# The first net's fifth chunk made by seven block products, and activations dealt without steps

## The chip, the cores and the metric

The kernel runs on one core of a Trainium2 chip. The metric is the device time of one execution in microseconds; what counts is the median over several runs. Five engines work side by side: TensorE (PE) multiplies matrices, VectorE (DVE) and ScalarE (ACT) do elementwise work, GpSimd (POOL) a little of everything, and SyncE (SP) issues nearly all loads from memory in one queue.

## The reference

Two layers of a mixed network over 256 tokens of width 1024, in float32. Each layer has two gated nets ("ffn1" and "ffn2"), a mixer and a cross attention, each with a layer norm behind it. The change is in the four gated nets.

```python
def swiglu(x, w_gate, w_up, w_down):
    return (jax.nn.silu(x @ w_gate) * (x @ w_up)) @ w_down

for l in range(DEPTH):                                       # DEPTH = 2
    h = layer_norm(ALPHA * h + 0.5 * swiglu(h, ffn1_gate[l], ffn1_up[l], ffn1_down[l]), ln_g[l, 0], ln_b[l, 0])
    ...                                                      # mixer: layer_norm(ALPHA * h + mix)
    h = layer_norm(ALPHA * h + cross_attn(h, mem, ...), ln_g[l, 2], ln_b[l, 2])
    h = layer_norm(ALPHA * h + 0.5 * swiglu(h, ffn2_gate[l], ffn2_up[l], ffn2_down[l]), ln_g[l, 3], ln_b[l, 3])
```

The gate and up weights are 1024 x 2816, the down weights 2816 x 1024.

## The kernel before

**Precision by parts.** Every float32 operand of a large product is split into a high part (rounded by a copy on ScalarE) and a low part (the difference, on VectorE): `split`, lines 60 to 62. A product is then three matrix products, high by high, high by low, low by high (`mm_rows`, line 130; each goes through `product`, line 106). A tile of 1024 weight elements per partition thus costs one copy and one subtraction (line 62) before PE can use it. There are eight buffers each for high and low weights ("whi", "wlo") and three for raw weights as loaded ("raw").

**A gated net** (`ffn`, from line 377). The 2816 hidden columns are made in six chunks, five of 512 and one of 256. For a chunk of 512, `hidden` makes all products of x with the gate weights and with the up weights: 2 tiles of 128 tokens x 8 blocks of 128 rows x 2 matrices x 3 parts = 96 products of 512 columns. `activate` (line 402) applies silu on ScalarE, `gated` (line 406) multiplies on VectorE. `turn` (line 410) brings the result, which has tokens on partitions, to hidden columns on partitions: four loads deal it from tile "sg" to tile "dealt" in groups of 32 partitions, and VectorE turns blocks of 32 x 32 (line 418), once for each tile of tokens, before they are split. The chunk's down products follow later: `both(c, u)` adds half u of chunk c, 24 products, to the sums in "dn". Behind chunk c come `both(c - 2, 1)` and `both(c - 1, 0)`; the last three halves are in `tail`, in front of the layer norm in `finish`.

**Seven products** (`by_seven`, line 515). In the second, third and fourth net, chunk 3 is made otherwise. Gate and up weights of the chunk form, with x, a product of 2 x 2 blocks, and this is made with seven block products of 12 instead of eight: 84 products of 512 columns. It needs sums of weight blocks (line 544, VectorE, in place, four sums of two pieces), each split as above, 14 splits in all; differences of the four quarters of x (`blocks_of_x`, lines 499 to 513), which are kept in the tiles of the attention's keys (kTh, kTl); and sums and differences of the results (`put`, line 566). The quarters and later block 00 of the weights lie in the tile "spare" of 2048 elements, block 01 in the tiles of the layer norm's scale and offset ("lng", "lnb"), blocks 11 and 10 in raw buffers. The quarters are made behind chunk 1, two chunks before they are used.

**The first net** has no chunk by seven (`sevens` is empty). Behind its chunk 1 it loads the small parameters and the cross attention's memory (`beginnings`, on POOL's queue), and behind its chunk 2 it turns the memory and computes with the parameters (`later`, lines 191 and 257); the tiles of the memory (tag "m") and of parameters are its own.

**Order of work.** Only a few stretches have an order written by hand: the start of the first net on PE, VectorE and ScalarE, and a part of the mixer. Elsewhere a planner goes through the instructions by the order in which the code emits them, and may take one that is ready earlier than one that is not; a tile is given to its next user when its last reader is done. `issue_after` queues a load or an instruction behind another one of its engine.

**Layouts of tokens.** `transposed` (line 173) turns h on PE with the unit matrix `idn`, or in one place `jdn`, which also reverses the tokens.

Of the kernel before, what the change touches and what calls it, by code (L numbers as in the profile page):

```python
# [46 lines left out]
def model(ctx: ExitStack, tc: tile.TileContext, t: dict, out: bass.AP):  # L47
# [16 lines left out]
    def load(src, k0, nk, c0, ncol, fine=False, strewn=False):  # L64

# [4 lines left out]
        for a in range(k0, k0 + nk, step):  # L70
# [4 lines left out]
            for b in range(0, step, part):  # L75
                loads.append(nc.sync.dma_start(
                    raw[:, b : b + part, :],
                    src[:, c0 : c0 + ncol].rearrange("(p k) c -> p k c", p=P)[:, a + b : a + b + part, :]
                    if strewn
                    else src[(a + b) * P : (a + b + part) * P, c0 : c0 + ncol].rearrange("(k p) c -> p k c", p=P),  # L80
                ))
# [71 lines left out]

    jdn = cst.tile([P, P], F32, name="jdn")
# [24 lines left out]
    def load_memory(mp, behind):  # L179
        m = [mp.tile([P, 4, 8, 32], F32, tag="m", name="m", bufs=2) for _ in range(2)]  # L180
# [23 lines left out]
    rows = cst.tile([P, P], F32, name="rows")  # L204
# [10 lines left out]
    def small_parameters(op):  # L215
        nc.gpsimd.memset(rows, 0.0)
# [13 lines left out]
        mf = op.tile([P, NT, len(narrow), 64], F32, name="mf", bufs=1)  # L230
# [61 lines left out]
    def finish(mm, y, scale, gb, last=False, flip=False):  # L292
# [6 lines left out]
        for i in range(NT):  # L299
# [8 lines left out]
            for c in pieces:  # L308
                n = c.start // 512
                v = halves(h[i][:, c])  # L310
                if len(pieces) == 3 and n:
                    o = acc((P, 256))
                    mm(i, n, slice(c.start - 512, c.stop - 512), o, None)
                    nc.vector.tensor_tensor(v, v, sums(o), op=ALU.add)  # L314
                else:
                    mm(
                        i, n, slice(0, 512), None,
                        None if last or not i or not n else lambda: transposed(h[0], 0, xTh, xTl),
                    )
                    nc.vector.scalar_tensor_tensor(v, v, ALPHA / scale, sums(y[i][n]), op0=ALU.mult, op1=ALU.add)  # L320
# [19 lines left out]
        return lambda: transposed(h[1], 1, xTh, xTl, jdn if flip else idn)  # L340

    def project_back(slabs, late, gb, scale, between=lambda: None):
# [30 lines left out]
        return finish(tail, y, scale, gb)  # L373


    def ffn(l, name, n, pend=None, last=False, early=None):
        gate, up, down = (t[f"{name}_{x}"][l] for x in ("gate", "up", "down"))
        with tc.tile_pool(name="ffn", bufs=2, reuse_waits="tile") as fp:
# [21 lines left out]

            def activate(s, i, og):
                nc.scalar.activation(halves(s[:, i, :]), sums(og), AF.Silu)

            def gated(s, i, ou):
                v = halves(s[:, i, :])
                nc.vector.tensor_tensor(v, sums(ou), v, op=ALU.mult)
# [4 lines left out]
            def turn(s):  # L411
# [4 lines left out]
                for i in range(NT):  # L416
                    d = fp.tile([P, 4, P], F32, tag="up", name="square")
                    nc.vector.transpose(  # L418
                        d.rearrange("p k (i b) -> p b k i", b=4), x[:, :, i, :].rearrange("p b (j k) -> p b k j", k=4)
# [4 lines left out]
            def first():  # L424
# [5 lines left out]
                if pend is None:  # L430
# [8 lines left out]
                    with tc.manual_schedule(engines={E.Activation, E.DVE, E.PE}):  # L439
# [8 lines left out]
                        transposed_half(h[0], 0, 0, xTh, xTl)  # L448
                        busy(1)
                        split(*wg.todo[0])  # L450
                        transposed_half(h[0], 0, 1, xTh, xTl)
# [3 lines left out]
                        transposed_half(h[1], 1, 0, xTh, xTl)  # L455
                        group(1, 0)
                        split(*wg.todo[2])
                        transposed_half(h[1], 1, 1, xTh, xTl)
# [56 lines left out]
            def by_seven(c0, bx):  # L515
                def quarter(m, j, halves_of):
                    for b, r in enumerate(halves_of):
                        n = r.shape[1]
                        k = 4 * j + b * n
                        loads.append(nc.sync.dma_start(  # L520
                            r, m[k * P : (k + n) * P, c0 : c0 + CHUNK].rearrange("(k p) c -> p k c", p=P)
                        ))
                    return [r[:, 2 * h : 2 * h + 2, :] for h in range(2) for r in halves_of[:1]] if n == 4 else halves_of

# [3 lines left out]
                def raw():  # L528
                    return rows_by_columns(wp.tile([P, 2048], F32, tag="raw", name="raw", bufs=3))

                w00 = quarter(gate, 0, [rows_by_columns(
                    fp.tile([P, 4, 4 * P], F32, tag="spare", name="sum", bufs=1).rearrange("p n c -> p (n c)")
                )])
                w01 = quarter(up, 0, [
                    rows_by_columns(wp.tile([P, DM], F32, tag=g, name="raw")) for g in ("lng", "lnb")
                ])
                w11 = quarter(up, 1, [raw()])
                w10 = quarter(gate, 1, [raw()])

                def parts_of(r, plus=None):  # L540
                    hi, lo = [], []
                    for i in range(2):
# [4 lines left out]
                        h, w = (x.rearrange("p (k c) -> p k c", c=CHUNK) for x in (h, w))  # L547
# [14 lines left out]
                def half_sum():  # L562
                    return halves(fp.tile([P, 4, P], F32, tag="up", name="half").rearrange("p k t -> p (k t)"))

                def put(o, a, op, b):
                    nc.vector.tensor_tensor(o, a, b, op=op)

                s = activations()
                g = [halves(s[:, i, :]) for i in range(NT)]
                o = [acc((P, CHUNK)) for _ in range(4)]  # L570
                run(o[0], part_of_x(0, 0), parts_of(w00))
                nc.scalar.copy(g[0], sums(o[0]))
# [3 lines left out]
                put(e, sums(o[1]), ALU.add, g[0])  # L576
                run(o[3], bx[2], parts_of(w01, w11))
                put(g[1], sums(o[3]), ALU.add, e)
                f = half_sum()
                put(f, sums(o[2]), ALU.subtract, g[1])  # L580
                put(e, sums(o[2]), ALU.subtract, e)
# [4 lines left out]
                m = acc((P, CHUNK))  # L586
                run(m, part_of_x(1, 1), parts_of(w00, w10))
                put(g[1], sums(m), ALU.add, g[1])
                nc.scalar.activation(g[1], g[1], AF.Silu)
                put(g[1], g[1], ALU.mult, f)  # L590
                m = acc((P, CHUNK))
                run(m, bx[3], parts_of(w11))
                put(e, sums(m), ALU.add, e)
                put(g[0], g[0], ALU.mult, e)
                return turn(s)

            def last_hidden(c0):
# [11 lines left out]
                split(ah[:, 0:2, :], al[:, 0:2, :], s)  # L609
                return ah, al  # L610

            def slab(c, u):
                if c < len(chunks) - 1:
                    w = load(down[c * CHUNK : (c + 1) * CHUNK], 2 * u, 2, 0, DM, strewn=True)
                else:
                    w = load(down, c * 4, 2, 0, DM)
# [4 lines left out]
            sevens = (3,) if early is None else ()  # L621
# [17 lines left out]
            for c, (c0, ncol) in enumerate(chunks):  # L639
# [33 lines left out]
            return finish(tail, ys, 0.5, gb, last=last, flip=name == "ffn1")  # L673
# [27 lines left out]
    def mixer(l, fill):  # L701
        w_in = t["w_in"][l]
        with tc.tile_pool(name="mix", bufs=1, reuse_waits="tile") as mp:
# [284 lines left out]
            return project_back([slab(a) for a in (0, 6, 2, 4)], 3, gb, 1.0)  # L988


    def attention(l, pend):
        scale = (DM // HEADS) ** -0.5
        with tc.tile_pool(name="att", bufs=1, reuse_waits="tile") as ap:
# [108 lines left out]
            return project_back([slab(a) for a in (0, 2, 4, 6)], 3, gb, 1.0, others)  # L1102
# [40 lines left out]
```

## Time and profile before

| | us |
|---|---|
| median of 3 runs | 1081.59 (1081.54 to 1081.89) |
| profiled execution | 1082.44 |
| its span | 1080.7 |
| PE busy in it | 1071.4 |
| VectorE busy | 908.4 |
| ScalarE busy | 592.8 |

The profile shows one execution. "PE" lines are matrix products; a product of 512 columns is shown with about 380 ns, but the next one starts 216 ns after it, since they are pipelined. "busy" in a window is the time in which at least one instruction of the engine ran. In a line of a group, the two figures behind the bar are the total busy time and the mean duration in ns; then come idle time in front of the group and who ended it. Line numbers are those of the kernel before.

### The profile page before, as it was taken

How to read it: one execution, taken by the hardware profiler on the slowest of the kernel's cores; microseconds unless marked ns; L12 is line 12 of the kernel's file. 1: busy time of each engine (PE TensorE's matmuls, PEld its weight loads, DVE VectorE, ACT ScalarE, POOL GpSimd, SP SyncE). 2: the span in 40 equal slices, each digit the busy share in tenths (PEclk: the TensorE clock that was granted, in tenths of full speed). 3: DMA queues.
4: the chain of work that ended last, by engine and by line, in shares of the span. 5: the costliest groups of instructions: out<-in, count | busy, mean ns of one | idle time of the engine just before them, and what ended most of it. 6: DMA issues, size and time to landing. Idle time of an engine off the chain costs nothing.

```text
span 1080.7 us, 15689 instructions
## 1 busy us (share of the span) xinstructions
PE 1071.4 (99%) x6015; PEld 947.5 (88%) x6015; DVE 908.4 (84%) x1198; ACT 592.8 (55%) x828; POOL 61.0 (6%) x113
## 2 busy tenths in 40 slices
PE   9999999999999999999999999999999999999997
PEld 7888888989899888888888888898898998888886
DVE  6678677998988898998697998798989889889885
ACT  6456553766457455556365465456764664645650
POOL 9500001000000000000000000010000000000000
PEclk9999999999999999999999999999999999999999
DMA  9986764754476387288468459656536664773761
GB/s 325 289 293 203 249 223 153 237 196 165 167 263 204 123 295 269 96 275 286 156 234 282 166 166 329 229 165 241 174 122 231 240 228 154 255 253 109 260 236 39
DMA packets 122715, 231.86 MB, mean 215 GB/s; under 512 B 6352, under 2 KB 45552, under 8 KB 117520
## 3 DMA queue, kind: packets, MB, share of 16 engines
q1 hardware_dynamic: 120848, 228.48, 63.1%
q0 software_dynamic: 1216, 1.20, 0.4%
q10 hardware_dynamic: 576, 1.18, 0.3%
q8 instruction: 47, 0.77, 0.3%
q14 instruction: 28, 0.23, 0.1%
HBM read 216.15 MB, written 1.05 MB: 201 GB/s over the span
## 4 chain that ended last, share of the span: by engine, by line
PE 99%; DMA 0%; DVE 0%; issue 0%; DVEq 0%
PE acc L106 65%; PE dn L106 30%; PE acc L170 1%; PE dn L845 1%; DMA h<-in_x_dram 0%; PE dn L904 0%; PE dn L903 0%; PE dn L893 0%; PE acc L969 0%; PE dn L810 0%; PE dn L437 0%; DVE h L334 0%; DVE h L330 0%; DVE st L322 0%; DVE h L314 0%
## 5 line engine op out<-in xcount | busy, mean ns | idle before, releaser
L62 DVE TENSOR_TENSOR wlo<-raw,whi 128x1024 fp32r<-128x1024 f32 (+1 forms) x390 | 460.8, 1207 | 91.0 <-ACT whi L61 81.1
L61 ACT CAST whi<-raw 128x1024 fp32r<-128x1024 f32 (+1 forms) x390 | 391.2, 1040 | 258.3 <-PE dn L106 128.4
L106 PE MATMUL acc<-whi,xT 128*128 128x512 f32 x1192 | 359.7, 380 | 0.0
L106 PEld LDWEIGHTS acc<-whi,xT 128*128 128x128 f32 x1192 | 225.2, 189 | 32.1
L106 PE MATMUL acc<-wlo,xT 128*128 128x512 f32 x596 | 225.9, 379 | 0.0
L106 PE MATMUL acc<-xT,whi 128*128 128x512 f32 x576 | 142.1, 382 | 0.0
L106 PE MATMUL dn<-whi,ah 128*128 128x512 f32 x346 | 131.5, 380 | 0.0
L106 PE MATMUL dn<-wlo,ah 128*128 128x512 f32 x346 | 131.2, 379 | 0.0
L106 PE MATMUL dn<-whi,al 128*128 128x512 f32 x346 | 131.1, 379 | 0.0
L106 PEld LDWEIGHTS acc<-wlo,xT 128*128 128x128 f32 x596 | 112.7, 189 | 15.7
L106 PEld LDWEIGHTS acc<-xT,whi 128*128 128x128 f32 x576 | 104.1, 190 | 11.8
L106 PE MATMUL dn<-whi,xT 128*128 128x512 f32 x288 | 88.8, 382 | 0.0
L106 PEld LDWEIGHTS acc<-xT,wlo 128*128 128x128 f32 x576 | 75.5, 191 | 3.9
L106 PE MATMUL acc<-xT,wlo 128*128 128x256 f32 x576 | 75.9, 275 | 0.0
L106 PEld LDWEIGHTS dn<-wlo,ah 128*128 128x128 f32 x346 | 65.4, 189 | 9.5 <-DVE wlo L62 0.3
L106 PEld LDWEIGHTS dn<-whi,al 128*128 128x128 f32 x346 | 65.4, 189 | 9.3
L106 PEld LDWEIGHTS dn<-whi,ah 128*128 128x128 f32 x346 | 65.4, 189 | 9.1
L418 DVE STREAM_TRANSPOSE square<-dealt 128x512 f32<-128x512 f32 x40 | 62.8, 1645 | 3.8 <-DMA dealt<-sg 3.8
L327 POOL TENSOR_TENSOR rs<-rs,nhalf 128x1 f32<-128x1 f32 x16 | 14.9, 928 | 846.3 <-DVE rs L326 846.3
L106 PEld LDWEIGHTS dn<-whi,xT 128*128 128x128 f32 x288 | 54.7, 190 | 7.8 <-DVE xT L62 0.3
L106 PE MATMUL dn<-wlo,xT 128*128 128x512 f32 x144 | 54.8, 381 | 0.0
L61 ACT CAST ah<-square 128x512 fp32r<-128x512 f32 x40 | 24.6, 619 | 39.7 <-DVE square L418 39.7
(227 smaller groups left out, 1174.0 us busy)
## 6 DMA issues: line engine op xcount, KB each, us to landing
raw<-in_ffn_down_dram SPq DMA_DIRECT2D x44, 1024.0 KB, 5.4
raw<-in_ffn_up_dram SPq DMA_DIRECT2D x41, 1024.0 KB, 6.1
raw<-in_ffn_gate_dram SPq DMA_DIRECT2D x39, 1024.0 KB, 5.1
raw<-in_w_in_dram SPq DMA_DIRECT2D x24, 1024.0 KB, 5.0
dealt<-sg SPq DMA_DIRECT2D x80, 128.0 KB, 3.8
raw<-in_ca_k_dram SPq DMA_DIRECT2D x8, 1024.0 KB, 4.9
raw<-in_w_out_dram SPq DMA_DIRECT2D x8, 1024.0 KB, 4.8
raw<-in_ca_v_dram SPq DMA_DIRECT2D x8, 1024.0 KB, 5.4
```

Of the source, the lines that this page charges most:

```text
L61: nc.scalar.copy(hi, src)
L62: lows.append(nc.vector.tensor_tensor(lo, src, hi.bitcast(F32), op=ALU.subtract))
L106: nc.tensor.matmul(o, w, x, start=start, stop=stop)
L170: nc.tensor.transpose(pt[:, k, :], src[:, (4 * j + k) * P : (4 * j + k + 1) * P], unit)
L327: nc.gpsimd.tensor_tensor(rs, rs, nhalf[:, 0:1], op=ALU.pow)
L418: nc.vector.transpose(d.rearrange("p k (i b) -> p b k i", b=4), x[:, :, i, :].rearrange("p b (j k) -> p b k j", k=4))
L845: nc.tensor.matmul(o[g, hh, :], kc[:, hh, g], x, start=True, stop=True)
```

## The change

1. Chunk 4 of the first net is made by seven products too. The quarters of x for it are made behind chunk 3. The layer norm's scale and offset are loaded behind chunk 5 there, since block 01 uses their tiles.
2. Three tiles of 1024 elements, "spare0" to "spare2", take the place of the tile "spare", the two of the memory and those of the parameters. The quarters and block 00 lie in "spare0" and "spare1"; block 10 lies in "dealt" and "spare2" and no longer in a raw buffer. Every block is loaded as two pieces of 512 KB. The products with blocks 11 and 10 change places, and the gated result of such a chunk is written to "spare2".
3. The silu and the gating write their result with groups of 32 columns in the order in which they are dealt, in two instructions for each tile of tokens where there was one; dealing and turning then read and write 32 elements in a row where they went in steps of four. The down weights are loaded in whole blocks of 128 rows, without the interleaving (`strewn`) that answered to those steps.
4. In exchange the tokens of a tile stand in another order within a net: x is turned with `pdn`, a permuted unit matrix, which POOL copies from `idn` at the start; behind a first net of a layer `jdn` and `idn` are used as before. The chunk of 256 is brought to the same order in its split, in two instructions each where there was one.

```diff
-    def load(src, k0, nk, c0, ncol, fine=False, strewn=False):
+    def load(src, k0, nk, c0, ncol, fine=False):
...
+    pdn = cst.tile([P, P], F32, name="pdn")
+    nc.gpsimd.tensor_copy(pdn.rearrange("p (r b) -> p b r", b=4), idn.rearrange("p (b r) -> p b r", b=4))
...
-        m = [mp.tile([P, 4, 8, 32], F32, tag="m", name="m", bufs=2) for _ in range(2)]
+        m = [
+            mp.tile([P, DM], F32, tag=f"spare{n}", name="m", bufs=1).rearrange("p (k b j) -> p k b j", k=4, j=32)
+            for n in range(2)
+        ]
...
+            def ordered(v):
+                return v.rearrange("p (a k j) -> p k a j", a=4, j=32)
+
+            def by_two(v, o):
+                o = o.rearrange("p (n a j m) -> p m n a j", n=2, a=4, m=2)
+                return [(ordered(v)[:, 2 * m : 2 * m + 2], o[:, m]) for m in range(2)]
+
             def activate(s, i, og):
-                nc.scalar.activation(halves(s[:, i, :]), sums(og), AF.Silu)
+                for v, o in by_two(s[:, i, :], og):
+                    nc.scalar.activation(v, o, AF.Silu)
 
             def gated(s, i, ou):
-                v = halves(s[:, i, :])
-                nc.vector.tensor_tensor(v, sums(ou), v, op=ALU.mult)
+                for v, o in by_two(s[:, i, :], ou):
+                    nc.vector.tensor_tensor(v, o, v, op=ALU.mult)
...
                     nc.vector.transpose(
-                        d.rearrange("p k (i b) -> p b k i", b=4), x[:, :, i, :].rearrange("p b (j k) -> p b k j", k=4)
+                        d.rearrange("p k (b r) -> p b k r", b=4), x[:, :, i, :].rearrange("p b (k j) -> p b k j", k=4)
                     )
...
-                d = fp.tile([P, 4, 4 * P], F32, tag="spare", name="quarters", bufs=1)
-                q = [d[:, n, :].rearrange("p (k t) -> p k t", t=P) for n in range(4)]
+                d = [fp.tile([P, DM], F32, tag=f"spare{n}", name="quarters", bufs=1) for n in range(2)]
+                q = [d[n // 2].rearrange("p (n k t) -> p n k t", n=2, t=P)[:, n % 2] for n in range(4)]
...
+                w00 = block(gate, 0, pieces("spare0", "spare1"))
+                w01 = block(up, 0, pieces("lng", "lnb"))
+                w11 = block(up, 1, whole())
+                w10 = block(gate, 1, pieces("dealt", "spare2"))
...
-                m = acc((P, CHUNK))
-                run(m, part_of_x(0, 1), parts_of(w10))
-                put(g[0], sums(m), ALU.add, g[0])
-                nc.scalar.activation(g[0], g[0], AF.Silu)
...
+                o = [acc((P, CHUNK)) for _ in range(3)]
+                run(o[0], bx[3], parts_of(w11))
+                put(e, o[0], ALU.add, e)
+                run(o[1], part_of_x(0, 1), parts_of(w10))
+                put(g[0], o[1], ALU.add, g[0])
+                run(o[2], part_of_x(1, 1), parts_of(w00, w10))
+                put(g[1], o[2], ALU.add, g[1])
+                s = fp.tile([P, NT, CHUNK], F32, tag="spare2", name="sg", bufs=1)
+                for i, u in enumerate((e, f)):
+                    v = ordered(s[:, i, :])
+                    nc.scalar.activation(v, g[i].rearrange("p (k a j) -> p k a j", a=4, j=32), AF.Silu)
+                    nc.vector.tensor_tensor(v, v, u.rearrange("p (k a j) -> p k a j", a=4, j=32), op=ALU.mult)
...
-            sevens = (3,) if early is None else ()
+            sevens = (3,) if early is None else (4,)
...
-                if c == 1 and sevens:
+                if sevens and c == (1 if early is None else min(sevens) - 1):
                     bx = blocks_of_x()
                 if c == (max(sevens) + 1 if sevens else 1):
-
-                    with tc.issue_after(loads[-1].ins) if early is not None else nullcontext():
-                        gb = ln_params(l, n)
-                        rest = early(fp) if early is not None else ()
+                    gb = ln_params(l, n)
+                if c == 1 and early is not None:
+
+                    with tc.issue_after(loads[-1].ins):
+                        rest = early(fp)
```

More of the change, by code (lines that the diff above doesn't have):

```diff
@@ L215, in small_parameters @@
     def small_parameters(op):
+        spare = op.tile([P, DM], F32, tag="spare2", name="rows", bufs=1)
+        rows = spare[:, 0:P]
         nc.gpsimd.memset(rows, 0.0)
@@ L290, in ln_params, with finish @@
         return g, b
-    def finish(mm, y, scale, gb, last=False, flip=False):
+    def finish(mm, y, scale, gb, units, last=False):
         g, b = gb
@@ L317, in finish @@
                         i, n, slice(0, 512), None,
-                        None if last or not i or not n else lambda: transposed(h[0], 0, xTh, xTl),
+                        None if last or not i or not n else lambda: transposed(h[0], 0, xTh, xTl, units[0]),
                     )
@@ L339, in finish, with project_back @@
                     e.dma_start(out[0, tok(i), c], h[i][:, c])
-        return lambda: transposed(h[1], 1, xTh, xTl, jdn if flip else idn)
-    def project_back(slabs, late, gb, scale, between=lambda: None):
+        return lambda: transposed(h[1], 1, xTh, xTl, units[1])
+    def project_back(slabs, late, gb, scale, unit, between=lambda: None):
         y = [[acc((P, 512), "dn") for _ in range(2)] for _ in range(NT)]
```

94 lines of the change are left out of this document (40 added, 54 removed).

## The prediction

> **What bounds the kernel now.** I read the engine totals first, then the chain that ended last, then the chain in order of time.
>
> ```profile
> span 1080.7 us, 15689 instructions
> PE 1071.4 (99%) x6015; PEld 947.5 (88%) x6015; DVE 908.4 (84%) x1198; ACT 592.8 (55%) x828; POOL 61.0 (6%) x113
> ```
> ```profile
> 107.95 10.36 PE dn L106 x48
> 118.31 20.72 PE acc L106 x96
> 139.03 10.36 PE dn L106 x48
> ...
> 450.92 18.13 PE acc L106 x84
> ...
> 639.45 10.56 PE dn L106 x48
> ```
>
> TensorE (PE) is the whole chain. In 118.31 to 139.03, the first net's chunk 4, 96 products take 20.72 us, 0.216 us each; the chunk by seven products in the second net, at 450.92, has 84 and takes 18.13 us, the same 0.216 us. So nothing is gained unless PE gets fewer products, and everything else costs only where it makes PE wait. The one wait behind a chunk by seven is in the third net: its 48 products at 639.45 take 10.56 us where 10.36 is usual.
>
> Who could make PE wait is seen in the windows of the same stages (each engine: busy us, and count):
>
> ```profile
> 86.20:107.95 21.75, 21.75 (x102) 19.06 (x101) 21.04 (x37) 15.88 (x20) 0.00 (x0) 1.00 0.53 185
> 107.95:118.31 10.36, 10.36 (x50) 9.07 (x49) 7.51 (x7) 4.36 (x5) 0.00 (x0) 1.00 0.97 319
> 118.31:139.03 20.72, 20.72 (x98) 18.14 (x97) 12.47 (x13) 10.27 (x12) 0.00 (x0) 1.00 0.60 200
> 433.95:450.92 16.97, 16.97 (x80) 14.88 (x79) 16.87 (x16) 6.31 (x6) 0.00 (x0) 1.00 0.30 93
> 450.92:469.05 18.13, 18.13 (x85) 15.88 (x85) 18.13 (x20) 11.44 (x14) 0.00 (x0) 1.00 0.48 160
> ```
>
> The third pair of figures is VectorE (DVE). During a chunk by seven it works 18.13 of 18.13 us, and before it 16.87 of 16.97 us: it starts on the chunk's weights 17 us ahead of PE and only just arrives. In the first net it is free for 0.71 us in 86.20 to 107.95, for 2.85 in 107.95 to 118.31, and for 8.25 in 118.31 to 139.03. So the question is whether the first net's DVE can get its work done before PE asks for it.
>
> **The products.** 96 products become 84: -2.59 us on the chain, sure as far as PE is fed.
>
> **DVE per operation.** The rows by shape (busy us, mean ns):
>
> ```profile
> L418 DVE STREAM_TRANSPOSE square<-dealt 128x512 f32<-128x512 f32 x40 | 62.8, 1645 | 3.8 <-DMA dealt<-sg 3.8
> L544 DVE TENSOR_TENSOR sum<-sum,raw 128x1024 f32<-128x1024 f32 x18 | 21.5, 1221 | 0.2
> L406 DVE TENSOR_TENSOR sg<-acc,sg 128x512 f32<-128x512 f32 x34 | 22.4, 683 | 0.0
> L127 DVE TENSOR_TENSOR sums<-acc,sums 128x256 f32<-128x256 f32 x32 | 13.3, 419 | 2.5 <-ACT sums L126 2.5
> L980 DVE STREAM_TRANSPOSE yr<-dealt 128x512 f32<-128x512 f32 x4 | 4.7, 1287 | 0.0
> L1054 DVE STREAM_TRANSPOSE square<-dealt 128x512 f32<-128x512 f32 x6 | 4.2, 705 | 0.0
> L503 DVE TENSOR_TENSOR quarters<-xT 128x512 f32<-128x512 f32 x12 | 7.9, 681 | 0.0
> ```
>
> The turning (L418) steps by four elements on both sides and takes 1645 ns. After the change both sides run 32 elements in a row, as in L1054, which takes 705 ns; L980, with one side stepped, takes 1287. I take 705, and 1287 as the bound: two turns per chunk give back 1.9 us of DVE (0.7 at the bound). The gating (L406) goes from two instructions of 683 ns to four of half the size, each about the 419 of L127: +0.3 us per chunk. The same split on ScalarE adds two activations per chunk; it is busy 10.27 of 20.72 us, so nothing. In the three later nets all of this falls where PE is dense already; it can only remove the 0.2 us at 639.45. I count -0.2, with 0 and -0.5 as ends.
>
> **The first net, as a ledger of DVE time.** Where its work stands when chunk 4 comes:
>
> ```profile
> 98.04 0.69 DVE L195 STREAM_TRANSPOSE turned<-m 128x512 f32<-128x512 f32 x1
> ...
> 102.75 3.50 DVE L62 TENSOR_TENSOR wlo<-raw,whi 128x1024 fp32r<-128x1024 f32 x3 [0.43 <-ACT whi L61]
> 106.53 1.22 DVE L62 TENSOR_TENSOR wlo<-raw,whi 128x1024 fp32r<-128x1024 f32 x1 [0.29 <-ACT whi L61]
> ```
> ```profile
> 105.45 1.06 ACT L61 CAST whi<-raw 128x1024 fp32r<-128x1024 f32 x1 [0.83 <-PE acc L106]
> 108.05 1.05 ACT L61 CAST whi<-raw 128x1024 fp32r<-128x1024 f32 x1 [1.54 <-PE acc L106]
> ```
> ```profile
> 383.07 1.28 DVE L503 TENSOR_TENSOR quarters<-xT 128x512 f32<-128x512 f32 x2
> ...
> 462.99 2.34 DVE L62 TENSOR_TENSOR wlo<-raw,whi 128x1024 fp32r<-128x1024 f32 x2
> ```
>
> Three in a row take 3.50 us, so one weight split costs 1.14 at the pace of a full queue, and an addition of the same shape (L544) as much; two L503 in a row take 1.28, so an operation of that shape costs 0.60. The casts wait for PE to give back one of eight weight buffers. At 107.95, when PE begins the down products, four buffers hold their weights and four are for chunk 4; the cast at 108.05 is the fourth of these, so the split at 106.53 was chunk 4's third. Before 107.95 the DVE can therefore spare these three splits (3.4 us), its 0.7 us of idleness, and 1.8 us from the two turns of chunk 2 (it sits within 86.20 to 107.95): 5.9 us. Nothing else there can be put off: the memory's turnings (L195), up to 98.7, must even come first, since the first net's quarters of x now lie in the tiles that the memory was loaded into.
>
> The last weights of the chunk are wanted when half of its seventh product is done: 118.31 + 6.5 x 2.59 = 135.15. That is 27.2 us after 107.95; with the 5.9, DVE has 33.1 us. It must do in it: twelve operations for the quarters of x, their differences and splits, 12 x 0.60 = 7.2 (new in this net, and emitted only after chunk 3); 14 splits and 8 additions of weight blocks, 22 x 1.14 = 25.1; chunk 3's gating, four halves at some 0.36, 1.4; chunk 3's two turns and splits, 2 x 0.63 + 2 x 0.60 = 2.5; and two of the sums that free accumulators, 1.2. Together 37.4. It is 4.3 us short, so PE waits 4.3 us by the seventh product. (In the second net, where the quarters of x are made long before, the last two splits of the chunk end at 465.33, and PE wants them at 450.92 + 6.5 x 2.59 = 467.76: 2.4 us ahead.)
>
> Behind that the DVE holds seven more small operations of this chunk, at 0.60, among the two splits that the next down block needs, where PE has no lead left: about 1 us more. Afterwards a down block asks 2.3 us of DVE per 5.18 us of PE, and the backlog drains. So the waits are 5.3 us, the products save 2.6, the later nets 0.2: **+2.5 us**.
>
> The ends: with DVE kept perfectly in order (chunk 3's two splits and half of the small sums put off) the shortage is 2 to 3 us and the net 0. For the other end, weight block 00 now lies in the tiles of the quarters and can be fetched only when they are done, about 107.5:
>
> ```profile
> raw<-in_ffn_up_dram SPq DMA_DIRECT2D x6, 512.0 KB, 4.0
> sum<-in_ffn_gate_dram SPq DMA_DIRECT2D x3, 1024.0 KB, 7.3
> ```
>
> At 4.0 us for half a block it arrives at 111.5, just as DVE runs out of other work; at 7.3 it arrives at 114.8, DVE loses 3 us more, and the net is +5.5.
>
> **What costs nothing, and what covers it.**
>
> ```profile
> 1.19 0.30 POOL masks.py:199 TENSOR_SCALAR_AFFINE_SELECT idn<-idn 128x128 f32<-128x128 f32 x1
> ...
> 4.66 1.09 PE L170 MATMUL acc<-idn,h 128*128 128x128 f32 x4 [0.63 <-DMA h<-in_x_dram]
> ...
> 420.29 0.39 SPq L520 DMA_DIRECT2D sum<-in_ffn_gate_dram  x1
> ```
>
> The loads of a chunk by seven become eight of 512 KB; SP's queue issues one in about 0.4 us. The half of block 10 in "dealt" waits in that queue for the turns of the chunk before, and holds the loads behind it; it is wanted only five products (13 us) into the chunk, and such a load lands in 4.0. The first net's scale and offset of the norm are fetched at chunk 5 rather than chunk 1; they are used behind that chunk's products, which begin at 149.4, and block 01 leaves their tiles by some 130. The down weights, now in whole blocks of 128 rows, keep their 1 MB per load. The permutation on POOL (a copy of 128 by 128) precedes the first turning on PE, which waits for x until 4.66; POOL has its unit matrix by 1.5, so up to 3 us are covered, and beyond that each us would be one of PE. The last block's split in two adds under 0.2 us per net, where DVE has 8 us free per chunk.
>
> **Clock.** A wait has a second price:
>
> ```profile
> 7.68 0.63 PE L106 MATMUL dn<-whi,xT 128*128 128x512 f32 x1
> 8.10 0.63 PE L106 MATMUL dn<-wlo,xT 128*128 128x512 f32 x1
> ```
>
> At the start of the program PE's products begin 0.42 us apart, not 0.216. No wait inside the kernel is long enough to show whether this comes back. The Trainium skill (TensorE: Matmul & The Clock Gate, What's actually happening) says that it does: after an idle window of about 3.4 us the array runs at half clock until it has been busy for about as long. My 5.3 us come in parts: nothing until the third product, whose first weights (both additions of block 00, then the split) are about 2.8 us late, about 2.2 before the fifth, and the rest, so the sum is made without a slow spell.
>
> **The rivals.** (A, the forecast, 0.50) The DVE backlog costs PE more than the 12 products give: +2.5 us, own range 0 to +5.5.
>
> (B, 0.26, faster) The backlog never reaches PE. The order of each engine's work is set by a planner, not by the text; if it lets PE run the next down blocks (24 products, 5.18 us each, for 2.3 us of DVE) ahead of late block products, PE has 10.36 us more to do in which DVE catches up 4.3 or more. For it: the raw buffers that the chunk no longer uses are free for those loads. Against it: in every net PE's groups stand in the order of the text (48, 84, 48 above), and DVE is full, so the down splits are not ready sooner. It gives -2.6 - 0.2 = -2.8.
>
> (C, 0.18, no difference) Half of that: one down block, or the small sums put off, covers 2.5 to 3 of the 5.3 us. -0.5 to +0.5.
>
> (D, 0.06, slower) The late block 00 and the shortage gather into one wait, and PE falls back to the pace of the program's start, 0.42 instead of 0.216 us per product. For one of the seven block products that adds 12 x 0.20 = 2.4 us, for two 4.9; with 3.3 between them, A's +2.5 becomes +5.8. It decides from a gap longer than any that the rows show (0.2 us at 639.45). By the page's 3.4 us the gap would have to be that long, and sixteen products would be slow: the same 3.3 us, an estimate.
>
> That the turning is not quicker is part of A: at 1287 ns it adds 1.4 us to the shortage.
>
> **The numbers.** The profiled execution took 1082.44 us (span 1080.7 and 1.7 around it), 0.85 above the median of the runs, 1081.59. With +2.5: 1084.9 against the first, 1084.1 against the median, which I predict. A reaches from 1081.6 to 1087.1, B is at 1078.8, C 1081.1 to 1082.1, D 1087.4. The range from 1078.8 to 1087.1 leaves out about 1 in 6: D, and the tails of A and B. What this kernel's measurement can tell from no change is 0.2%, 2.16 us: A is slower beyond that in about 0.40 of its 0.50 and within it in 0.10; B is faster; C is the same; D slower. So faster 0.26, same 0.28, slower 0.46.
>
> **What would show it.** Right: 6003 PE instructions; turnings near 700 ns; the first net's 84 products spread over 22 us or more, with PE waiting for DVE's weight splits; DVE without a gap from about 86 to 145; block 00's load issued after 105. Wrong: the first net's 84 products in 18.13 us and the next group at 136.4 (B), PE's down products in between (B or C), or products at 0.42 us apart after a wait (D). If the turns stay near 1.6 us, or if DVE finishes the seven blocks early, the ledger is wrong.

## The result, and the profile after

The changed kernel takes 1092.49 us (median of 4 runs, 1092.11 to 1094.11) where the kernel before takes 1081.74 in the same session: a ratio of 1.0102, 95% interval 1.0085 to 1.012. The forecast was 2.5 us slower with 1087.1 as the upper end; it became 10.75 us slower. The profiled execution took 1092.11 us.

The head of the page after:

```profile
span 1090.3 us, 15813 instructions
...
PE 1072.6 (98%) x6003; PEld 944.1 (87%) x6003; DVE 906.8 (83%) x1267; ACT 606.9 (56%) x875; POOL 62.1 (6%) x114
```

PE has the twelve products less (6003 for 6015), and the span is 9.6 us longer. The windows of two stages, the down products in front of chunk 4 and the chunk itself (the third pair of figures is DVE, the fourth ACT):

```profile
107.10:117.46 10.36, 10.36 (x49) 9.07 (x49) 5.71 (x9) 1.04 (x1) 0.00 (x0) 1.00 0.78 238
117.46:148.29 30.83, 23.02 (x85) 16.05 (x85) 29.43 (x31) 16.97 (x20) 0.00 (x0) 0.94 0.27 88
```

The 84 products of chunk 4 take 30.83 us in place of 18.13: 12.7 us in which PE waits or runs slowly. Before, the 96 products took 20.72. The stage is 10.1 us longer; it begins 0.85 us earlier, and all the rest adds up to 0.3. So the whole loss is in this one place. What PE waited for, from the view of the waits (us in total, times, longest):

```profile
PE acc L103 <- ACT whi L61: 5.9, 7, 2.1
PE acc L103 <- DVE wlo L62: 1.9, 3, 1.0
```

It waited for the parts of the weights. This view counts 7.8 us. The rest of the 12.7 is not idle time by it: six products at 0.42 (last section) cost about 1.2 us, and the idle time in front of a product is counted from the end of the one before, 0.38 us after that one's start, where a fed PE begins the next after 0.216. Both parts of the weights come late, and DVE stands behind both. DVE's timeline in these stages (start, duration, and in brackets the idle time in front and who ended it):

```profile
110.62 1.22 DVE L62 TENSOR_TENSOR wlo<-raw,whi 128x1024 fp32r<-128x1024 f32 x1 [1.48 <-ACT whi L61]
111.88 2.48 DVE L561 TENSOR_TENSOR raw<-raw 128x1024 f32<-128x1024 f32 x2
117.91 1.30 DVE L433 STREAM_TRANSPOSE square<-dealt 128x512 f32<-128x512 f32 x2 [3.54 <-DMA dealt<-sg]
...
120.84 2.36 DVE L62 TENSOR_TENSOR wlo<-raw,whi 128x1024 fp32r<-128x1024 f32 x2 [0.25 <-ACT whi L61]
...
145.66 1.23 DVE L62 TENSOR_TENSOR wlo<-raw,whi 128x1024 fp32r<-128x1024 f32 x1 [0.59 <-ACT whi L61]
```

DVE's last split of the chunk ends at 146.89. PE wants it 6.5 block products into a stage that begins at 117.46, at 134.3: it is 12.6 us late, and five products later the stage is over. Between 107.1 and 146.9 DVE is idle for 5.86 us (the four brackets), 5.0 of it before 117.91, just where it had the most to catch up on. The queue of SP and the timeline of ACT say why:

```profile
103.81 0.37 SPq L547 DMA_DIRECT2D raw<-in_ffn_gate_dram  x1
107.23 0.37 SPq L75 DMA_DIRECT2D raw<-in_ffn_down_dram  x1
109.17 3.48 SPq L430 DMA_DIRECT2D dealt<-sg  x4
113.01 6.61 SPq L547 DMA_DIRECT2D raw<-in_ffn_gate_dram  x2
```
```profile
109.54 1.04 ACT L61 CAST whi<-raw 128x1024 fp32r<-128x1024 f32 x1 [2.82 <-DMA raw<-in_ffn_gate_dram]
118.65 1.21 ACT L61 CAST ah<-square 128x512 fp32r<-128x512 f32 x2 [8.06 <-DVE square L433]
119.77 1.99 ACT L61 CAST whi<-raw 128x1024 fp32r<-128x1024 f32 x2
```

The first half of block 00 is fetched at 103.81, when the quarters have left the first tile. The second half is fetched at 113.01 only: the dealing of chunk 3 stands ahead of it in SP's queue. The dealing, beside the 1 MB load issued at 107.23, lands late (7.1 us from issue by the view of the transfers in this stretch), DVE stands in front of the turning for 3.54 us, and ACT stands behind that turning for 8.06 us with the next casts of weights in its queue.

What the change was to make quicker did become quicker:

```profile
L433 DVE STREAM_TRANSPOSE square<-dealt 128x512 f32<-128x512 f32 x40 | 26.0, 687 | 6.2 <-DMA dealt<-sg 6.2
L420 DVE TENSOR_TENSOR sg<-acc,sg 128x256 f32<-128x256 f32 x64 | 23.1, 414 | 0.0
```

Turning takes 687 ns where it took 1645. In the third net the 48 products behind the chunk by seven take 10.36 us again, where they took 10.56.

### The profile page after: what moved, and what is told of

The parts are those of the page before. It is cut to its first block, busy times and chain, and to the rows that moved or that the text cites. A ratio compares the mean times of both kernels' runs of the same rounds, so it can differ in the third digit from the quotient of the medians.

```text
span 1090.3 us, 15813 instructions
## 1 busy us (share of the span) xinstructions
PE 1072.6 (98%) x6003; PEld 944.1 (87%) x6003; DVE 906.8 (83%) x1267; ACT 606.9 (56%) x875; POOL 62.1 (6%) x114
## 4 chain that ended last, share of the span: by engine, by line
PE 93%; DVE 4%; DMA 1%; issue 1%; ACT 1%; SPq 0%; DVEq 0%; ACTq 0%
PE acc L103 61%; PE dn L103 29%; DVE wlo L62 2%; PE acc L170 1%; DMA dealt<-sg 1%; PE dn L863 1%; DVE raw L561 1%; ACT whi L61 0%; DMA h<-in_x_dram 0%; PE dn L922 0%; DVE kTl L62 0%; DVE quarters L518 0%; DVE half L583 0%; DVE quarters L526 0%; SPq L430 0%
## 5 line engine op out<-in xcount | busy, mean ns | idle before, releaser
L62 DVE TENSOR_TENSOR wlo<-raw,whi 128x1024 fp32r<-128x1024 f32 (+1 forms) x420 | 496.9, 1209 | 106.4 <-ACT whi L61 96.9
L61 ACT CAST whi<-raw 128x1024 fp32r<-128x1024 f32 (+1 forms) x420 | 421.5, 1041 | 276.1 <-PE dn L103 114.2
L103 PE MATMUL acc<-whi,xT 128*128 128x512 f32 x1152 | 349.6, 381 | 3.1 <-ACT whi L61 3.1
L103 PEld LDWEIGHTS acc<-whi,xT 128*128 128x128 f32 x1152 | 218.0, 189 | 34.9 <-ACT whi L61 4.1
L103 PE MATMUL acc<-wlo,xT 128*128 128x512 f32 x576 | 219.2, 381 | 1.9 <-DVE wlo L62 1.9
L103 PEld LDWEIGHTS acc<-wlo,xT 128*128 128x128 f32 x576 | 109.1, 189 | 18.5 <-DVE wlo L62 3.2
L103 PEld LDWEIGHTS acc<-xT,whi 128*128 128x128 f32 x576 | 104.1, 190 | 11.8
L324 DVE SCALAR_TENSOR_TENSOR h<-h,dn 128x512 f32<-128x512 f32 x31 | 21.1, 682 | 27.4 <-PE dn L103 27.4
L103 PE MATMUL acc<-whi,mT 128*128 128x512 f32 x128 | 40.2, 380 | 0.0
```

What stands on the lines that cost most here:

```text
L61: nc.scalar.copy(hi, src)
L62: lows.append(nc.vector.tensor_tensor(lo, src, hi.bitcast(F32), op=ALU.subtract))
L103: nc.tensor.matmul(o, w, x, start=start, stop=stop)
```

## The experiments

Three theories stood against each other: that DVE has too much work in one stretch (the quarters of x among it), that block 00 comes too late, and that the other parts of the change, or a fall of PE's clock, cost something of their own. The kernel before took 1081.60 to 1081.65 us in the sessions of all of them.

**Everything but the seven products.**

```diff
-            sevens = (3,) if early is None else (4,)
+            sevens = (3,) if early is None else ()
```

> The changed kernel with the first net's chunk 4 made as before, by 96 products; all else of the change stays (dealing without steps, the permuted tokens, the shared tiles, block 10 in other tiles). Theory (the whole loss is in the first net's chunk by seven, where VectorE is late): 1081.3 to 1081.6 us, 0 to 0.3 below the kernel before. Rival (the rest of the change costs too, by its doubled instructions or by SP's queue): 1083 or more.

Measured: 1081.72 us (1081.58 to 1082.04), ratio 0.9999 [0.9989, 1.0008]. The permutation, the new tiles, the pieces of 512 KB and the finer gating cost nothing that shows, and the quicker turning gains nothing that shows. All of the loss belongs to chunk 4 made by seven.

**The quarters of x in tiles of their own, made early.** In the first net the tiles of the norm's scale and offset are empty until block 01 comes, so the quarters can lie there from the start and need not wait for the memory.

```diff
-                d = [fp.tile([P, DM], F32, tag=f"spare{n}", name="quarters", bufs=1) for n in range(2)]
+                places = ((fp, "spare0"), (fp, "spare1")) if early is None else ((wp, "lng"), (wp, "lnb"))
+                d = [p.tile([P, DM], F32, tag=g, name="quarters", bufs=1) for p, g in places]
...
-                if sevens and c == (1 if early is None else min(sevens) - 1):
+                if sevens and c == 1:
```

> The quarters of x are made in the tiles of the norm's scale and offset in the first net, and behind chunk 1, so that they need not wait for the memory's tiles; block 00 needs only the memory's turning. Theory (VectorE starts on the chunk too late because the quarters and block 00 stand behind the memory): 7.2 us of VectorE work leave the crowded stretch and block 00 arrives by about 104; PE's waits fall from 12.7 us to 0 to 3, so 1079.5 to 1083. Rival (VectorE has too much to do however early it starts, since eight weight buffers limit its lead): waits stay above 5 us, 1085 or more.

Measured: 1079.52 us (1079.2 to 1080.94), ratio 0.998 [0.997, 0.999]. The loss is gone and the gain of the products is there.

**The same tiles, emitted as late as in the change** (the first two lines of that diff alone).

> As the one with early quarters in the tiles of scale and offset, but made behind chunk 3 as in the changed kernel. If it is the shared tiles that delay the quarters, the planner can take them in any gap before, and the time is that of the early quarters (within 1 us). If it is their place in the text, they stay in 95 to 108 us and the time is within 2 us of the changed kernel, 1090 to 1093.

Measured: 1079.48 us (1079.39 to 1080.99), ratio 0.9979 [0.997, 0.9989]: the place in the code makes no difference. A line of DVE's timeline, then the chain in order of time, then the windows of the same two stages:

```profile
39.25 0.69 DVE L62 TENSOR_TENSOR kTl<-quarters,kTh 128x512 fp32r<-128x512 f32 x1
```
```profile
107.23 10.36 PE dn L103 x48
117.59 18.13 PE acc L103 x84
135.72 10.57 PE dn L103 x48
```
```profile
107.23:117.59 10.36, 10.36 (x50) 9.10 (x49) 10.33 (x13) 4.19 (x4) 0.00 (x0) 1.00 0.21 51
117.59:135.72 18.13, 18.13 (x86) 15.92 (x85) 17.54 (x21) 13.77 (x16) 0.00 (x0) 1.00 0.43 146
```

With nothing in the way of the tiles, the planner makes the quarters between 8.7 and 39.9 us, while DVE has time. Block 00 is fetched before 96, and DVE works 10.33 of 10.36 us in front of the chunk, where it worked 5.71. Work emitted late was done early, once its tile was free: the shared tile, not the line in the code, put twelve operations into the crowded stretch.

**Block 00 fetched through POOL's queue**, past the dealing in SP's queue.

```diff
+                        q = nc.gpsimd if early is not None and m is gate and j == 0 else nc.sync
-                        loads.append(nc.sync.dma_start(
+                        loads.append(q.dma_start(
```

> The two loads of block 00 in the first net go through POOL's queue, not SP's; nothing else changes. Theory (the second half of block 00 came at 118.6 because its load stood in SP's queue behind the dealing of chunk 3): it lands 5 us sooner, VectorE's 3.5 us of idleness before 117.9 is partly filled, 1087 to 1090. Rival (VectorE's own order, in which the turning of chunk 3 stands first and waits for its dealing, holds it anyway): 1091.5 to 1093.

Measured: 1091.28 us (1090.83 to 1093.59), ratio 1.009 [1.0075, 1.0105]: between the two expectations, nearer to the rival's, and only 1.2 us less than the change. Two answers of the view of the transfers, for the second half of block 00 and for the stretch from 104 to 120 us (KB, median us from issue to landing), and ACT's timeline:

```profile
raw<-in_ffn_gate_dram POOLq DMA_DIRECT2D x1, 512.0 KB, 7.2
```
```profile
raw<-in_ffn_down_dram SPq DMA_DIRECT2D x1, 1024.0 KB, 4.9
dealt<-sg SPq DMA_DIRECT2D x4, 128.0 KB, 6.8
```
```profile
116.24 2.00 ACT L61 CAST whi<-raw 128x1024 fp32r<-128x1024 f32 x2 [6.29 <-PE dn L103]
```

The second half is issued at 108.95, four microseconds earlier, but now it moves beside the dealing and a load of down weights and needs 7.2 us: it lands at 116.15, and its cast begins at 116.24. (The view names a down product that ended just then as the releaser; the landing is as close.) DVE is idle for 3.59 us in front of its split, as long as it stood for the dealing in the change. Out of the queue, the load met the transfers that had stood ahead of it.

**Block 00 and block 01 with their tiles exchanged:** block 00 comes early, the quarters still lie in the tiles of the memory and are made late; block 01 takes their place.

```diff
-                w00 = block(gate, 0, pieces("spare0", "spare1"))
-                w01 = block(up, 0, pieces("lng", "lnb"))
+                mine, other = ("spare0", "spare1"), ("lng", "lnb")
+                if early is not None:
+                    mine, other = other, mine
+                w00 = block(gate, 0, pieces(*mine))
+                w01 = block(up, 0, pieces(*other))
```

> The changed kernel, but in the first net block 00 lies in the tiles of scale and offset and block 01 in the tiles of the quarters. Block 00 can be loaded early; the quarters stay where they were, at 95 to 108 us, so VectorE has the same work. Theory (what bound the changed kernel is when block 00 arrives; the amount of VectorE work comes second): the waits fall from 12.7 us to the shortage of the ledger and a little, 5 to 8, so 1084.5 to 1087.5. Rival (the quarters' 7.2 us in the crowded stretch are the cause): 1090 to 1092.5.

Measured: 1088.8 us (1088.56 to 1090.79), ratio 1.0069 [1.0054, 1.0084], between the two expectations. From DVE's timeline:

```profile
118.50 1.30 DVE L433 STREAM_TRANSPOSE square<-dealt 128x512 f32<-128x512 f32 x2 [2.12 <-DMA dealt<-sg]
...
142.52 1.23 DVE L62 TENSOR_TENSOR wlo<-raw,whi 128x1024 fp32r<-128x1024 f32 x1 [0.59 <-ACT whi L61]
```

The quarters fill 95 to 108 as in the change, DVE stands for the dealing for 2.12 us, and otherwise it is full to the end.

**Block 00 late, the quarters early:** the tiles of the second experiment, and block 00's loads queued behind the dealing of chunk 3.

```diff
-                w00 = block(gate, 0, pieces("spare0", "spare1"))
+                with tc.issue_after(deals[-1].ins) if early is not None else nullcontext():
+                    w00 = block(gate, 0, pieces("spare0", "spare1"))
```

> The opposite: quarters in the tiles of scale and offset, made early as in the faster kernel, but the loads of block 00 are queued in SP behind the dealing of chunk 3, so that they are issued at about 112 us as in the changed kernel. Theory (block 00's arrival binds): VectorE can begin on the chunk only at 117 and the time is that of the changed kernel or 2 us less, 1089 to 1093. Rival (VectorE's amount of work binds): 1079.5 to 1084.

Measured: 1091.36 us (1091.21 to 1091.45), ratio 1.0088 [1.0073, 1.0103]: nearly the whole loss, without one operation for the quarters in the stretch.

```profile
105.83 0.76 DVE L420 TENSOR_TENSOR sg<-acc,sg 128x256 f32<-128x256 f32 x2 [4.95 <-PE acc L103]
107.12 0.76 DVE L420 TENSOR_TENSOR sg<-acc,sg 128x256 f32<-128x256 f32 x2 [0.54 <-PE acc L103]
113.18 1.30 DVE L433 STREAM_TRANSPOSE square<-dealt 128x512 f32<-128x512 f32 x2 [5.30 <-DMA dealt<-sg]
116.12 1.22 DVE L62 TENSOR_TENSOR wlo<-raw,whi 128x1024 fp32r<-128x1024 f32 x1 [0.25 <-ACT whi L61]
...
144.48 1.23 DVE L62 TENSOR_TENSOR wlo<-raw,whi 128x1024 fp32r<-128x1024 f32 x1 [0.59 <-ACT whi L61]
```

Here DVE simply has nothing to do for 11.6 us. Against the third experiment either cause alone costs 9 to 12 us, and both together 13: they do not add, since the quarters are made in the time in which DVE would stand waiting for block 00. One account fits all four kernels: DVE's time lost between 95 us and its last split of the chunk (idle, or spent on the quarters at 0.60 us each), against how late that split and the kernel end. The chunk starts within 0.2 us of 117.5 in all four, so the ends are compared as they stand; differences are to the third experiment. The end of the third experiment's chunk, in DVE's timeline and in PE's:

```profile
130.64 0.68 DVE L584 TENSOR_TENSOR sg<-acc,half 128x512 f32<-128x512 f32 x1
131.24 1.22 DVE L62 TENSOR_TENSOR wlo<-raw,whi 128x1024 fp32r<-128x1024 f32 x1
...
133.57 1.22 DVE L62 TENSOR_TENSOR wlo<-raw,whi 128x1024 fp32r<-128x1024 f32 x1
```
```profile
134.48 0.38 PE L103 MATMUL acc<-wlo,xT 128*128 128x512 f32 x1
```

The product at 134.48, the fifth from the end of the chunk, is the first that needs the last low part. It begins before the split at 133.57 has ended (134.79), so that one belongs to the next down block, and the chunk's last split ends at 132.46.

| kernel | quarters | idle | lost more | last split ends | later | median, later |
|---|---|---|---|---|---|---|
| third experiment | 0 | 0.59 | | 132.46 | | |
| tiles exchanged | 7.2 | 2.71 | 9.3 | 143.75 | 11.3 | 9.3 |
| block 00 late | 0 | 11.63 | 11.0 | 145.71 | 13.2 | 11.9 |
| the change | 7.2 | 5.86 | 12.5 | 146.89 | 14.4 | 13.0 |

The median follows the time lost within 1 us. The last split is some 2 us later still: in the third experiment two of the six sums that free accumulators stand in front of it (at 128.22 and 130.64), in the other three kernels all six, four more at 0.60. In return the third experiment has about 2 us in hand, for PE wants that split at 117.59 + 6.5 x 2.59 = 134.4. The two cancel, so that here a microsecond of DVE lost is about a microsecond of the kernel. That they cancel is luck of these kernels and no rule. Block 00 through POOL's queue lies on the same line: quarters 7.2, idle 4.83, so 11.4 lost more, and a median 11.8 later.

**The steps kept:** the kernel before, with its stepped dealing and turning, and with the first net's seven products alone (the quarters in the norm's tiles, the memory in the tile "spare").

```diff
-                d = fp.tile([P, 4, 4 * P], F32, tag="spare", name="quarters", bufs=1)
-                q = [d[:, n, :].rearrange("p (k t) -> p k t", t=P) for n in range(4)]
...
+                    d = [wp.tile([P, DM], F32, tag=g, name="quarters") for g in ("lng", "lnb")]
...
-            sevens = (3,) if early is None else ()
+            sevens = (3,) if early is None else (4,)
```

> The kernel before with the seven products in the first net alone: dealing and turning in steps as before, block 10 in a raw buffer, the quarters in the tiles of scale and offset, the memory in the tile of the quarters. VectorE has 1.9 us more to turn per chunk, less 0.3. If the dealing without steps was needed for the chunk to keep up: PE waits 1 to 3 us in the first net, 1080.5 to 1082.5. If not: 1079.3 to 1079.9.

Measured: 1081.82 us (1080.6 to 1083.02), ratio 1.0 [0.9991, 1.001]. PE waits once in the first net's chunk, for a sum that frees an accumulator:

```profile
PE acc L106 <- DVE half L574: 1.3, 1, 1.3
```
```profile
120.15 3.16 DVE L422 STREAM_TRANSPOSE square<-dealt 128x512 f32<-128x512 f32 x2
```

Two turns take 3.16 us where they took 1.30. This kernel is 2.3 us slower than the third experiment (1081.82 against 1079.48); its profiled execution, 1080.88, is one of its faster ones, and the one wait of 1.3 us covers its difference. The slower turning takes 1.86 us out of the about 2 us that the third experiment has in hand, which fits. But this kernel also keeps the loads of 1 MB, block 10 in a raw buffer and the old order of the products, so it is not shown that the turning alone is worth the 2.3 us. What is shown: the seven products in the first net gain nothing without the rest of the change, and the rest gains nothing without them (first experiment).

**Two chunks by seven in each of the later nets,** on the third experiment's kernel.

```diff
-            sevens = (3,) if early is None else (4,)
+            sevens = (2, 4) if early is None else (4,)
```

> The faster kernel with two chunks by seven (2 and 4) in each of the three later nets, where it has one; the first net keeps its one. 36 products fewer in all, 7.8 us of PE. If VectorE keeps up (each chunk by seven asks about 21 us more of it than one of 96 products, and one chunk of 96 lies between): 1071.7 to 1074. If it does not: the waits eat the gain, 1077 or more.

Measured: 1097.49 us (1097.19 to 1100.67), ratio 1.0144 [1.0127, 1.0161].

```profile
PE acc L103 <- ACT whi L61: 6.4, 3, 2.1
PE acc L103 <- DVE wlo L62: 6.3, 12, 0.8
```

36 products fewer (7.8 us at 0.216), and still 18 us slower than the third experiment: PE waits for the weight parts of the second chunk by seven in each later net, 12.7 us by these two lines. Not all of the loss is waiting. Behind these waits PE's granted clock falls in all three nets, in the first of them so:

```profile
500.00:505.00 5.00, 4.75 (x11) 3.81 (x12) 4.15 (x6) 4.73 (x7) 0.00 (x0) 0.50 0.00 0
```

The 48 down products that follow take 11.80, 12.03 and 12.25 us in place of 10.36. How much of the 18 us would be left without the slow spells was not tried.

**PE kept busy in the gaps.** In the change PE's granted clock fell to 0.56 between 122.5 and 125 us (last section). Idle products, whose results are overwritten, were put into the first net's gaps.

```diff
+                def idle_products(o, n):
+                    if early is not None:
+                        for _ in range(n):
+                            nc.tensor.matmul(o, xTh[:, 0, 0:P], xT[:, 0].rearrange("p s t -> p (s t)"), start=True, stop=True)
...
-                run(o[0], part_of_x(0, 0), parts_of(w00))
+                run(o[0], part_of_x(0, 0), parts_of(w00), o[3], 9)
```

> The changed kernel with idle products added in the first net (nine behind the first half of the first block's product, four and three around the last block's), whose results are overwritten, so that TensorE has work in the gaps between 120 and 124 us in which its granted clock fell to 0.56. Nothing is left out. Theory: the products that the slow spell stretches would have stood waiting for VectorE's splits at about 126 us anyway, so keeping the clock up moves the wait and not the end: 1091.5 to 1092.7 us, with granted clock 1.00 in the stage. Rival: the slow spell is a term of its own, about 1.4 us by the eight products at 0.42 us in place of 0.22: 1090.3 to 1091.0 us.

Measured: 1092.97 us (1092.62 to 1095.16), ratio 1.011 [1.0093, 1.0127], 0.3 us above what the theory gave and well above the rival's 1091.0. The windows of this kernel from 120 us:

```profile
120.00:122.50 2.50, 1.76 (x8) 0.82 (x6) 2.25 (x4) 2.12 (x3) 0.00 (x0) 1.00 0.69 202
122.50:125.00 2.50, 2.47 (x11) 1.71 (x10) 2.50 (x3) 0.80 (x2) 0.00 (x0) 1.00 0.02 7
125.00:127.50 2.50, 0.96 (x2) 0.37 (x2) 2.50 (x3) 1.88 (x2) 0.00 (x0) 1.00 0.00 0
127.50:130.00 2.50, 1.84 (x6) 1.48 (x6) 2.50 (x3) 0.00 (x0) 0.00 (x0) 0.67 0.00 0
```

The clock stayed up between 120 and 127.5 and fell afterwards, behind the next gaps. So the test did what it should at the first place and not in the whole stage; the time did not come down. DVE's last split ends at 147.26, 0.4 us later than in the change; its turning had already begun 0.36 later. That the slow spell costs nothing where PE waits for DVE anyway agrees with this, but a stage free of slow spells was not had in this experiment. The kernel with block 00 late bears it out from the other side: its granted clock is 1.00 throughout the chunk, and it stands on the same line of the table.

```profile
117.50:147.10 29.60, 21.57 (x85) 14.87 (x85) 28.98 (x29) 15.11 (x17) 0.00 (x0) 1.00 0.22 72
```

## Why the prediction was wrong

The direction and the mechanism were right: DVE cannot feed the first net's chunk, and PE waits for its weight splits by more than the twelve products save. The size was wrong, 10.75 for 2.5 us, beyond the upper end.

- **The products.** -2.59 us, sure as far as PE is fed: right. Fed, the 84 products take 18.13 us (third experiment), and the kernel is 2.24 us faster than without them (1079.48 against 1081.72).
- **DVE per operation.** Turning at 705 ns: 687. Gating at 419: 414. The -0.2 us in the later nets: the third net's stage did lose its 0.2 us, but the first experiment's ratio of 0.9999 shows nothing of it.
- **The ledger.** It came out 4.3 us short, with 5.3 us of waits. Of the work, 31.5 us was to be done behind the start of the down products; it was 33.9 (39.8 us from 107.1 to 146.9, less 5.86 idle). The price of 1.14 per split and 0.60 per quarter held. Mis-sized were the sums that free accumulators: two were counted, six stand in front of the last split, 2.4 us more, of which the prediction had about 1 behind the end. Where DVE is not held up the ledger is right: without the quarters it has 30.2 us of work for 33.1, 2.9 in hand; in the third experiment the last split ends 2.0 us ahead of PE, with two such sums in front of it and 0.59 us idle.
- **The idle time, the step that failed.** The ledger put the time in which DVE stands still at nothing: "DVE without a gap from about 86 to 145" was one of its signs, and it is 5.86 us idle. Of this only the late block 00 was seen, as the upper end, +3 us at a landing of 7.3. The landing of its halves was near that (5.6 and 6.0 us), but the second was issued at 113.0 and not at 107.5, though its tile was free at 108.5: the prediction weighed SP's queue for the half of block 10, which waits there for a tile, and not the dealing of chunk 3 ahead of block 00. And it had the turnings wait for nothing, while the dealing took 7.1 us. Waits by this sum, made after the fact: 5.3 + 5.9 + 1.4 = 12.6, where 12.7 were measured.
- **Where the quarters are made.** The prediction gave two reasons for their coming late: they lie in the memory's tiles, and they are "emitted only after chunk 3". The third experiment shows that the tile alone decides.
- **What costs nothing** cost nothing that shows (first experiment).
- **The rivals.** B and C needed PE to take down products ahead of late block products; its groups stayed in the order 48, 84, 48. C's other way, the small sums put off, went the opposite way: they moved in front of the last split. D's slow pace did come, at 0.42 us per product behind a gap of 2.11 us, but not with D's price: it reckoned with up to 24 slow products, six came, and DVE was still behind when they were done.

## What to carry to other kernels

When two uses share a tile, look at what the second use feeds: here the sharing pushed twelve operations and one load into the stretch with the least slack, and moving them to tiles that stood empty turned a loss of 10.8 us into 2.2 us of gain, of the 2.6 that the products promise. A ledger of an engine's work has to have a column for the time in which it must stand still, with the in-order queues of the other engines and of the DMA issuer walked through in that stretch; where there is next to no slack, such time is paid for in the kernel. A saving on an engine off the chain (the quicker turning) shows nothing by itself, and may be worth its price once another change has used up that engine's spare time; the kernel with the steps kept fits that, but more than the turning differs in it.

## What the runs showed of the hardware

**The clock can fall behind short gaps.** PE's timeline in the change, in front of the six slow products and in them:

```profile
120.87 0.48 PE L103 MATMUL acc<-whi,xT 128*128 128x512 f32 x1 [2.11 <-ACT whi L61]
121.81 0.80 PE L103 MATMUL acc<-whi,kTh 128*128 128x512 f32 x1 [0.46 <-ACT whi L61]
122.40 0.63 PE L103 MATMUL acc<-wlo,xT 128*128 128x512 f32 x1
122.83 1.06 PE L103 MATMUL acc<-whi,xT 128*128 128x512 f32 x2
```

Two gaps of 2.11 and 0.46 us with one product between them, then products 0.42 us apart for 2.7 us. In the kernel with the exchanged tiles, shorter gaps did it, where PE then had work in plenty:

```profile
142.54 0.48 PE L103 MATMUL acc<-whi,xT 128*128 128x512 f32 x1 [0.94 <-ACT whi L61]
143.80 0.55 PE L103 MATMUL acc<-wlo,xT 128*128 128x512 f32 x1 [0.78 <-DVE wlo L62]
144.15 1.06 PE L103 MATMUL acc<-whi,xT 128*128 128x512 f32 x2
```

That profiled execution took 1090.79 us, the other three 1088.56 to 1089.0, and the change has the same two gaps (0.94 and 0.78 us, in front of 145.68 and 146.94) without a slow spell behind them. So what decides is not the single gap. In the kernel with two chunks by seven a gap of 2.14 us had a slow spell behind it in each of the three later nets. The Trainium skill (TensorE: Matmul & The Clock Gate, What's actually happening) has the clock depend on how busy PE was in a window of about 3.4 us that runs freely, and puts the half clock behind at least one idle window. That the same gaps are followed by a slow spell in one execution and not in another agrees with a window that runs freely. That it must be an idle window does not agree: in the 3.4 us in front of 143.80 PE had work for roughly half of the time.

**Small transfers beside large ones.** The four loads of 128 KB that deal a chunk took 3.1 us to land in the two kernels where no load was issued in the 5 us ahead of them (third experiment, and block 00 late), and 7.1 and 7.5 us in the change and with the exchanged tiles, where a load of 1 MB had been issued 2 us ahead of them. With the exchanged tiles:

```profile
raw<-in_ffn_down_dram SPq DMA_DIRECT2D x1, 1024.0 KB, 9.7
dealt<-sg SPq DMA_DIRECT2D x4, 128.0 KB, 7.5
```
